# Hybrid retention and MLA block: wide modulation sets, row-tile groups of 1, 3, 5 and 7, and the norm factor applied at PSUM evacuation

## The chip, the cores and the metric

One core of one Trainium2 chip runs the whole program. The metric is device time in microseconds of one execution; a smaller number is better. Three runs of the kernel before are known, and one further execution was profiled.

## What is computed

One encoder layer for 256 tokens of width 2048, all in float32. The parts that the change touches:

```python
mod = (c_act @ ada_w[l] + ada_b[l])[:, None, :]          # c_act = silu(c), ada_w 2048 x 12288
shift_a, scale_a, gate_a, shift_f, scale_f, gate_f = jnp.split(mod, 6, axis=-1)
h = rmsnorm(x, norm1_w[l]) * (1.0 + scale_a) + shift_a
proj = h @ w_in[l]                                       # 2048 x 5184
...                                                      # retention heads and MLA heads on proj
x = x + gate_a * (jnp.concatenate([ret_out, mla_out], axis=-1) @ w_o[l])
h = rmsnorm(x, norm2_w[l]) * (1.0 + scale_f) + shift_f
x = x + gate_f * ((jax.nn.silu(h @ w_gate[l]) * (h @ w_up[l])) @ w_down[l])
return rmsnorm(x, final_norm_w)
```

The six vectors of the modulation come from one token's conditioning, so a 2048 x 12288 matrix (100.7 MB) is read for six vectors. All weights together are some 305 MB, and each is read once.

## The kernel before, in words

**Streams.** All weights lie in one HBM tensor in the order of use, and the SP queue alone issues their loads. A weight step ("w", `split_weights`, L119 to L127) loads a slab into one of six "stg" buffers (512 KB), ScalarE rounds it to a high half `whi` (L124), VectorE subtracts to get the low half `wlo` (L126), three buffers each. TensorE then makes three float32r matmuls where one would do: L132 high x high, L133 high x low, L134 low x high (`mm_tokens`).

**Modulation.** `ada_set` makes a set of up to four tiles of 128 columns for one of the six sections (SC_A is scale_a, SH_A shift_a, GT_A gate_a, and so on). Its matrix slab comes in 512 KB loads through the same six "stg" buffers ("a" steps, L185). A set goes one of two ways: on TensorE (L196: c_act, padded to 32 columns, is the stationary operand, and the 16 row tiles go to four 32-partition strips of one bank), or on VectorE (L198 and L200: one multiply-add over 128 x 512 per row tile into `ada_acc`). `finish` adds a gate's bias row (L212), `spread` sums over partitions: a gate by a matmul with ones (L218), the others by transposes (L222) and a reduction (L226), then L227 and L230 make `mod` and the gain. The string ADA_PE chooses the way set by set for SC_A and SH_A, ADA_PE2 for the sets that are needed later.

**The front.** w_in has 16 row tiles of 128. They are taken in GROUPS of 2, 4, 4 and 6, since the shift and scale of a row tile are needed before `h` of that tile can be made: while group g is projected, the modulation of group g+1 is loaded, its steps spread evenly between the weight steps (L372 to L392; LEAD says how many weight steps remain behind the last of them). `norm_x` squares x (L266), makes the factor (`rsqrt`, L114), scales x in place (L269); `turn_x` transposes it (L148) and ScalarE copies it out of PSUM (L276). `build_h1` applies gain and shift and splits (L143 to L145). Each group's `project` runs over eleven chunks of columns (CHUNKS: two PSUM banks each) and adds the chunk into SBUF accumulators (L348 copies for the first group, L350 adds for the others).

**Behind it.** The last group's chunks, MLA, retention and the output projection follow in a plan (L742 to L786) into which the loads of GT_A and of most of SC_F and SH_F are mixed, at a rate that compares an assumed DMA cost with an assumed TensorE cost (ADA_RATE, L790 to L805). Then `norm_x2` spreads the second norm factor by a small matmul (L727), the remaining SC_F and SH_F are loaded beside the first ffn chunks, and the ffn runs to the end with GT_F's modulation in between.

**Order.** `run` (L152) walks the steps and emits the loads of up to LOOK + 1 steps ahead, weights and modulation counted together. The framework then puts the instructions of each engine in an order by this priority and by its own times, with buffers from the free ones of a pool; the order is fixed before the run. The pool "big" has eight slots of 1 MB for x, its transpose, the h tiles and later tensors.

Of the kernel before, what the change touches and what calls it, by code (L numbers as in the profile page):

```python
# [85 lines left out]
def encoder_block(ctx: ExitStack, tc: tile.TileContext, x, cols, rows, pos, stream, out):  # L86
# [65 lines left out]
    def run(steps):  # L152
        ahead = [i for i, s in enumerate(steps) if s[0] != "f"]
        tiles, nxt, held = {}, 0, 0
        for i, s in enumerate(steps):
            while s[-1] not in URGENT and nxt < len(ahead) and (ahead[nxt] <= i or len(tiles) + held <= LOOK):
                j = ahead[nxt]
                kind, arg = steps[j][:2]
                tiles[j] = split_weights(arg) if kind == "w" else arg()
                nxt += 1  # L160
            if s[0] == "f":
# [12 lines left out]
    def ada_set(pool, sec, k0, nk, rowdst, on_pe):  # L174
        n = nk * P
        wide = n if not on_pe else min(n, 2 * P)
        kk = 1024 // wide
        acc = {}

        def acc_tile():  # L180
            return (pool or late["pool"]).tile([P, n], F32, name="ada_acc", tag="ada_acc", bufs=2 if pool else 1, padded_shape=[P, 512])

        def load(c, t):
            w = wp.tile([P, kk, wide], F32, name="stg", tag="stg", bufs=6)
# [3 lines left out]
        def body(c, t, w):  # L188
            if c == 0 and t == 0:
                acc["t"] = bank() if on_pe else acc_tile()  # L190
            a = acc["t"]
            for j in range(kk):
# [4 lines left out]
                elif k == 0:  # L197
                    V.tensor_scalar(out=a, in0=w[:, j], scalar1=c_act[:, 0:1], scalar2=None, op0=ALU.mult)  # L198
                else:
                    V.scalar_tensor_tensor(out=a, in0=w[:, j], scalar=c_act[:, k:k + 1], in1=a, op0=ALU.mult, op1=ALU.add)  # L200

        def finish():
# [5 lines left out]
            if rowdst is not None:  # L208
                r0 = (R_GA if sec == GT_A else R_GF) + k0 * P
                br = wp.tile([1, n], F32, name="bias_row", tag="stg", bufs=6)  # L210
                SY.dma_start(br, rows[:, r0:r0 + n])
                V.tensor_tensor(a[0:1, :], a[0:1, :], br, op=ALU.add)  # L212

        def spread():
            a = acc["a"]
            b = bank()
            if rowdst is not None:
                PE.matmul(b[:, 0:n], lhsT=ones, rhs=a, start=True, stop=True)  # L218
                S.copy(rowdst()[:, k0 * P:k0 * P + n], b[:, 0:n])
                return  # L220
# [771 lines left out]
```

## Time and profile before

| what | us |
|---|---|
| median of 3 runs | 1261.68 (1259.57 to 1261.85) |
| the profiled execution | 1259.87 |
| its span, first to last instruction | 1257.9 |
| TensorE (PE) busy | 1217.3, 97% |
| VectorE (DVE) busy | 841.1, 67% |
| ScalarE (ACT) busy | 600.9, 48% |
| DMA | 315.28 MB, mean 251 GB/s |

PE is matmuls, PEld their weight loads, SP the engine that issues the DMAs. Matmuls overlap in the pipeline, so the distance between two starts, not a matmul's duration, is its price. Times within the trace count from the first instruction.

### The profile page before, as it was taken

The numbers are of one execution on the slowest core, as the hardware profiler recorded it, in microseconds if no ns is written. First come the engines' busy times: TensorE is split into PE (matmuls) and PEld (weight loads), VectorE is DVE, ScalarE is ACT, GpSimd is POOL, SyncE is SP. The second block draws the span as 40 slices with busy tenths as digits, with TensorE's granted clock in tenths as the row PEclk, the third lists the DMA queues.
The fourth block names the chain that finished last, engine by engine and source line by source line (L and its number), as shares of the span: only waits on it lengthen the run. The fifth ranks groups of instructions, "written<-read, shape, count | busy, mean of one in ns | idle before, by whom it ended". The sixth has DMA issues, their size and how long they took to land.

```text
span 1257.9 us, 16210 instructions
## 1 busy us (share of the span) xinstructions
PE 1217.3 (97%) x6022; PEld 973.0 (77%) x6022; DVE 841.1 (67%) x1157; ACT 600.9 (48%) x812; POOL 2.2 (0%) x10
## 2 busy tenths in 40 slices
PE   5899999999999999899999999999999999999997
PEld 2676667789886787678888888888888888888885
DVE  2596988889997997885555556656655454554544
ACT  4553454545557554745444444444444443444433
POOL 0000000000000000000000000000000000000000
PEclk9999999999999999899999999999999999999999
DMA  8989898888878987897676658766775655555562
GB/s 330 324 302 310 296 326 295 291 311 298 323 243 297 319 289 268 323 356 222 218 226 225 202 170 284 235 198 212 262 224 189 218 188 197 194 191 194 191 200 85
DMA packets 88800, 315.28 MB, mean 251 GB/s; under 512 B 10249, under 2 KB 10377, under 8 KB 88209
## 3 DMA queue, kind: packets, MB, share of 16 engines
q1 hardware_dynamic: 88720, 314.24, 73.4%
q8 instruction: 47, 0.77, 0.2%
q14 instruction: 33, 0.26, 0.1%
HBM read 312.11 MB, written 2.10 MB: 250 GB/s over the span
## 4 chain that ended last, share of the span: by engine, by line
PE 85%; DVE 7%; DMA 4%; ACT 2%; issue 2%; SPq 0%; ACTq 0%; DVEq 0%
PE bank L133 25%; PE bank L134 25%; PE bank L132 25%; DMA stg<-in_stream 4%; DVE wlo L126 3%; PE bank L196 3%; PE bank L148 2%; DVE ada_acc L200 2%; ACT whi L124 1%; PE bank L625 1%; PE bank L614 1%; PE bank L513 0%; PE bank L537 0%; PE bank L512 0%; PE bank L222 0%
## 5 line engine op out<-in xcount | busy, mean ns | idle before, releaser
L126 DVE TENSOR_TENSOR wlo<-stg,whi 128x1024 fp32r<-128x1024 f32 (+2 forms) x400 | 478.8, 1199 | 331.8 <-ACT whi L124 330.3
L124 ACT CAST whi<-stg 128x1024 fp32r<-128x1024 f32 (+2 forms) x400 | 413.2, 1034 | 526.1 <-PE bank L134 411.9
L132 PE MATMUL bank<-whi,actt 128*128 128x512 f32 (+1 forms) x1184 | 457.7, 392 | 11.4 <-ACT whi L124 8.2
L133 PE MATMUL bank<-wlo,actt 128*128 128x512 f32 (+1 forms) x1184 | 460.7, 389 | 6.9 <-DVE wlo L126 6.2
L134 PE MATMUL bank<-whi,actt 128*128 128x512 f32 (+1 forms) x1184 | 458.1, 387 | 0.2 <-DVE actt L145 0.2
L132 PEld LDWEIGHTS bank<-whi,actt 128*128 128x128 f32 x1184 | 221.8, 189 | 63.6 <-ACT whi L124 12.0
L133 PEld LDWEIGHTS bank<-wlo,actt 128*128 128x128 f32 x1184 | 223.2, 189 | 61.5 <-DVE wlo L126 16.7
L134 PEld LDWEIGHTS bank<-whi,actt 128*128 128x128 f32 x1184 | 223.1, 188 | 44.8 <-DVE actt L145 0.9
L200 DVE SCALAR_TENSOR_TENSOR ada_acc<-stg,c_act,ada_acc 128x512 f32<-128x512 f32 (+1 forms) x240 | 175.3, 731 | 21.2 <-DMA stg<-in_stream 18.3
L132 PE MATMUL bank<-whi,ap 128*128 128x512 f32 x352 | 137.0, 389 | 0.0
L134 PE MATMUL bank<-whi,ap 128*128 128x512 f32 x352 | 136.9, 389 | 0.0
L133 PE MATMUL bank<-wlo,ap 128*128 128x512 f32 x352 | 136.9, 389 | 0.0
L132 PEld LDWEIGHTS bank<-whi,ap 128*128 128x128 f32 x352 | 66.1, 188 | 13.8
L133 PEld LDWEIGHTS bank<-wlo,ap 128*128 128x128 f32 x352 | 66.1, 188 | 13.7
L134 PEld LDWEIGHTS bank<-whi,ap 128*128 128x128 f32 x352 | 66.1, 188 | 13.6
L196 PE MATMUL bank<-stg,c_pad 128*32 128x256 f32 x544 | 48.6, 418 | 11.4 <-DMA stg<-in_stream 11.3
L196 PEld LDWEIGHTS bank<-stg,c_pad 128*32 128x32 f32 x544 | 13.0, 112 | 35.5 <-issue 26.7
L851 ACT ACTIVATE sgs<-bank 128x512 f32<-128x512 f32 x22 | 13.1, 597 | 10.5 <-PE bank L134 9.8
L145 DVE TENSOR_TENSOR actt<-hfull,actt 128x256 fp32r<-128x256 f32 x40 | 16.3, 419 | 2.4 <-ACT actt L144 2.3
L853 DVE TENSOR_TENSOR sgs<-bank,sgs 128x512 f32<-128x512 f32 x22 | 14.3, 683 | 0.6 <-PE bank L134 0.6
L833 DVE TENSOR_TENSOR ap<-bank,ap 128x512 fp32r<-128x512 f32 x22 | 14.1, 682 | 0.0
L226 DVE TENSOR_REDUCE mod<-bank 128x4 f32<-128x512 f32 (+3 forms) x18 | 8.0, 444 | 8.9 <-PE bank L222 8.7
(219 smaller groups left out, 708.2 us busy)
## 6 DMA issues: line engine op xcount, KB each, us to landing
stg<-in_stream SPq DMA_DIRECT2D x568, 512.0 KB, 4.4
stg<-in_stream SPq DMA_DIRECT2D x16, 288.0 KB, 3.5
stg<-in_stream SPq DMA_DIRECT2D x8, 384.0 KB
xt<-in_x SPq DMA_DIRECT2D x2, 1024.0 KB
acc_cq<-in_x SPq DMA_DIRECT2D x8, 256.0 KB, 4.7
out<-x SPq DMA_DIRECT2D x8, 256.0 KB, 2.9
acc_k<-in_rows SPq DMA_DIRECT2D x1, 1024.0 KB, 7.5
fw<-in_rows SPq DMA_DIRECT2D x1, 1024.0 KB
```

What stands on the lines that cost most here:

```text
L124: S.copy(hi, stg)
L126: V.tensor_tensor(lo, stg, hi.bitcast(F32), op=ALU.subtract)
L132: PE.matmul(o, lhsT=ah, rhs=whi, start=first, stop=False)
L133: PE.matmul(o, lhsT=ah, rhs=wlo, start=False, stop=False)
L134: PE.matmul(o, lhsT=al, rhs=whi, start=False, stop=last)
L145: V.tensor_tensor(dst[:, k, T:2 * T], tmp, dst[:, k, 0:T].bitcast(F32), op=ALU.subtract)
L148: PE.transpose(b[:, j, tb * P:(tb + 1) * P], src, ident)
L196: PE.matmul(a[q:q + 32, c:c + wide], lhsT=c_pad[:, k], rhs=w[:, j], start=c == 0 and k < 4, stop=c + wide == n and k >= KT - 4)
L200: V.scalar_tensor_tensor(out=a, in0=w[:, j], scalar=c_act[:, k:k + 1], in1=a, op0=ALU.mult, op1=ALU.add)
L833: V.tensor_tensor(ap[:, ks, T:2 * T], b, ap[:, ks, 0:T].bitcast(F32), op=ALU.subtract)
L851: S.activation(sg, o[tb], AF.Silu)
L853: V.tensor_tensor(sg, o[tb], sg, op=ALU.mult)
```

## The change

GROUPS become 1, 3, 5 and 7 row tiles. In the first three groups the chunks are WIDE: 1024 columns (four PSUM banks) and one row tile per load. The modulation of the front is given set by set: SC_A goes to TensorE, SH_A to TensorE for the first four tiles and to VectorE for the other twelve, in sets of up to seven tiles. Behind the first tile's, its loads are 640 KB to 1 MB and use free slots of the pool "big", not "stg". The look-ahead counts weights (LOOK_W = 3) and modulation (LOOK_A = 1) by themselves. Later sets have 1024 columns where they go to VectorE, and of the 40 tiles needed later all but four go there; they are placed evenly over the plan's cost. x is loaded in four pieces and transposed raw; the factor is spread over a tile `rstd_b` and multiplied in as VectorE reads PSUM. A gate's bias row is loaded into the accumulator before the first multiply-add. The sums over partitions are matmuls with one column of ones.

```diff
-GROUPS = [(0, 2), (2, 4), (6, 4), (10, 6)]
-ADA_PE = "10010100101101"
-LEAD = [1, 1, 3, 3, 3, 3, 3]
-ADA_PE2 = "010000110000"
-ADA_RATE = 0.8
-ADA_AHEAD = 0
-LOOK = 3
+GROUPS = [(0, 1), (1, 3), (4, 5), (9, 7)]
+LEAD = [1, 2, 3]
+ADA_PE2 = "000100"
+ADA_END = 0.95
+LOOK_W = 3
+LOOK_A = 1
...
-    def ada_set(pool, sec, k0, nk, rowdst, on_pe):
+    def ada_set(pool, sec, k0, nk, rowdst, on_pe, large=False):
         n = nk * P
-        wide = n if not on_pe else min(n, 2 * P)
-        kk = 1024 // wide
+        wide = n if not on_pe else P * (2 - nk % 2)
+        kk = 1 << ((2048 if large else 1024) // wide).bit_length() - 1
...
-            w = wp.tile([P, kk, wide], F32, name="stg", tag="stg", bufs=6)
+            if large:
+                w = big.tile([P, D], F32, name="astg", tag="m8")[:, 0:kk * wide].rearrange("p (k n) -> p k n", k=kk)
+            else:
+                w = wp.tile([P, kk, wide], F32, name="stg", tag="stg", bufs=6)
...
+                if not on_pe and rowdst is not None:
+                    G.memset(acc["t"], 0.0)
+                    bias_row(acc["t"])
...
             for j in range(nk):
-                PE.transpose(b[:, j * P:(j + 1) * P], a[:, j * P:(j + 1) * P], ident)
+                PE.matmul(b[:, j:j + 1], lhsT=a[:, j * P:(j + 1) * P], rhs=ones[:, 0:1], start=True, stop=True)
             ks = slice(sec * KT + k0, sec * KT + k0 + nk)
             m = mod[:, ks]
-            parts = b[:, 0:n].rearrange("p (j q) -> p j q", q=P)
-            V.tensor_reduce(out=m, in_=parts[:, :, ::32] if on_pe else parts, axis=AX.X, op=ALU.add)
-            V.tensor_tensor(m, m, col[:, C_ADAB + ks.start:C_ADAB + ks.stop], op=ALU.add)
+            V.tensor_tensor(m, b[:, 0:nk], col[:, C_ADAB + ks.start:C_ADAB + ks.stop], op=ALU.add)
...
+    S.activation(stat[:, 60:61], ones[:, 0:1], AF.Sqrt)
...
+    def spread_rstd(r):
+        b = bank()
+        for tb in range(NB):
+            dg = mid.tile([P, P], F32, name="dg", tag="hfull", bufs=2)
+            V.tensor_scalar(out=dg, in0=ident, scalar1=r[:, tb:tb + 1], scalar2=None, op0=ALU.mult)
+            PE.matmul(b[:, tb * P:(tb + 1) * P], lhsT=ones, rhs=dg, start=True, stop=True)
+        S.copy(rstd_b, b[:, 0:T])
...
-        S.copy(xnT[k // 8][:, k % 8:k % 8 + 2, :], b)
+    def scale_x(k):
+        V.tensor_tensor(xnT[k // 8][:, k % 8:k % 8 + 2, :], raw.pop(k), rstd_b.unsqueeze(1).broadcast_to([P, 2, T]), op=ALU.mult)
...
+        by = 1 if sum(widths) > CH else 2
...
+    pe_sets = [
+        [(SC_A, 1, 3), (SH_A, 1, 3)],
+        [(SC_A, 4, 4), (SC_A, 8, 1)],
+        [(SC_A, 9, 4), (SC_A, 13, 3)],
+    ]
+    dve_sets = [[], [(SH_A, 4, 5)], [(SH_A, 9, 7)]]
...
-        chunks = WIDE if nk == 1 else CHUNKS
-        ws = [w for c in chunks for w in project(gi, *c)]
+        parts = [ada_stream(mid, [(*st, None, on_pe, True) for st in sets[gi]]) for sets, on_pe in ((pe_sets, True), (dve_sets, False))]
+        order = sorted((i / len(u), n, i) for n, u in enumerate(parts) for i in range(len(u)))
+        units = [parts[n][i] for _, n, i in order]
+        ws = [w for c in WIDE for w in project(gi, *c)]
...
-    early = [(GT_A, 4 * i, 4, lambda: gate_a) for i in range(4)]
-    early += [(sec, k, min(4, K_LATE - k), None) for sec in (SC_F, SH_F) for k in range(0, K_LATE, 4)]
+    early = [(GT_A, 8 * i, 8, lambda: gate_a) for i in range(2)]
+    early += [(sec, k, min(8, K_LATE - k), None) for sec in (SC_F, SH_F) for k in range(0, K_LATE, 8)]
...
-        for _ in range(2):
-            if units and dma < pe * ADA_RATE + ADA_AHEAD:
-                steps += units.pop(0)
-                pe += 0.5
-                dma += 1.5
+        want = min(len(units), int(len(units) * done / (ADA_END * sum(cost))))
+        for u in units[used:want]:
+            steps += u
+        used = want
```

## Rows read from the trace of the kernel before

**Rows 1.** The page's chain that ended last, by engine

```profile
PE 85%; DVE 7%; DMA 4%; ACT 2%; issue 2%; SPq 0%; ACTq 0%; DVEq 0%
```

**Rows 2.** Windows by stage: us, busy us of each engine, PEclk, DMA share, GB/s

```profile
2.00:23.60 21.60, 9.91 (x72) 2.55 (x72) 5.30 (x12) 9.12 (x15) 0.74 (x2) 1.00 1.01 397
23.60:72.00 48.40, 42.47 (x233) 28.98 (x234) 27.70 (x37) 29.01 (x47) 0.00 (x0) 0.96 0.85 299
72.00:135.00 63.00, 62.66 (x334) 47.54 (x334) 50.97 (x70) 25.67 (x32) 0.00 (x0) 1.00 0.91 313
135.00:209.00 74.00, 69.76 (x376) 49.47 (x375) 64.53 (x133) 36.63 (x50) 0.00 (x0) 1.00 0.89 311
209.00:505.00 296.00, 293.66 (x1728) 236.93 (x1727) 259.72 (x455) 167.97 (x300) 0.00 (x0) 1.00 0.84 292
505.00:560.00 55.00, 50.19 (x208) 38.20 (x209) 50.93 (x74) 31.66 (x45) 0.00 (x0) 0.94 0.92 339
560.00:1258.00 698.00, 688.67 (x3078) 569.32 (x3076) 381.96 (x381) 299.62 (x328) 0.00 (x0) 1.00 0.63 207
```

**Rows 3.** Timeline of the start: start us, us, engine, line, operation, count

```profile
2.11 11.06 SPq L185 DMA_DIRECT2D stg<-in_stream  x8
...
9.12 1.91 ACT L266 ACTIVATE sq<-xt 128x2048 f32<-128x2048 f32 x1 [0.50 <-DMA xt<-in_x]
...
12.88 2.48 DVE L269 TENSOR_SCALAR xt<-xt,stat 128x2048 f32<-128x2048 f32 x2
...
14.26 1.08 PE L196 MATMUL bank<-stg,c_pad 128*32 128x256 f32 x8 [0.20 <-DMA stg<-in_stream]
...
19.38 1.08 PE L196 MATMUL bank<-stg,c_pad 128*32 128x256 f32 x8 [0.20 <-DMA stg<-in_stream]
...
23.63 0.72 PE L132 MATMUL bank<-whi,actt 128*128 128x512 f32 x1 [1.80 <-ACT actt L144]
```

**Rows 4.** Waits of the SP queue: us in total, times, longest us

```profile
SPq L122 <- DVE wlo L126: 532.6, 280, 4.2
```

**Rows 5.** Timeline of PE: starts of matmuls, 9 and 24 apart; modulation at 499.76

```profile
30.07 0.29 PE L133 MATMUL bank<-wlo,actt 128*128 128x288 f32 x1
...
31.25 0.30 PE L133 MATMUL bank<-wlo,actt 128*128 128x288 f32 x1
...
204.02 0.39 PE L134 MATMUL bank<-whi,actt 128*128 128x512 f32 x1
...
209.46 0.39 PE L134 MATMUL bank<-whi,actt 128*128 128x512 f32 x1
...
499.76 1.93 PE L196 MATMUL bank<-stg,c_pad 128*32 128x256 f32 x32
```

**Rows 6.** Groups of DVE by shape, 135 to 209: count, busy us, mean ns, idle before

```profile
L126 DVE TENSOR_TENSOR wlo<-stg,whi 128x1024 fp32r<-128x1024 f32 x19 | 23.2, 1221 | 2.4 <-ACT whi L124 2.3
L200 DVE SCALAR_TENSOR_TENSOR ada_acc<-stg,c_act,ada_acc 128x512 f32<-128x512 f32 x13 | 9.7, 747 | 0.0
L200 DVE SCALAR_TENSOR_TENSOR ada_acc<-stg,c_act,ada_acc 128x256 f32<-128x256 f32 x15 | 7.2, 482 | 0.2
...
L126 DVE TENSOR_TENSOR wlo<-stg,whi 128x576 fp32r<-128x576 f32 x4 | 2.9, 756 | 0.0
L350 DVE TENSOR_TENSOR acc_g<-acc_g,bank 128x512 f32<-128x512 f32 x4 | 2.7, 687 | 0.1
...
L350 DVE TENSOR_TENSOR acc_ck<-acc_ck,bank 128x288 f32<-128x288 f32 x4 | 1.6, 447 | 0.0
...
L226 DVE TENSOR_REDUCE mod<-bank 128x4 f32<-128x512 f32 x1 | 0.7, 692 | 0.1
```

**Rows 7.** Tile ada_acc: duration min/median/max ns of the bias add

```profile
L212 DVE TENSOR_TENSOR ada_acc<-ada_acc,bias_row x8: 659/673/674, 240.8 to 951.8; 1x512 f32<-1x512 f32 x8
```

**Rows 8.** Line L350: what its engine waited for before it, us and times

```profile
  PE bank L134: 12.2, 10
```

More of the change, by code (lines that the diff above doesn't have):

```diff
@@ L152, in run @@
     def run(steps):
-        ahead = [i for i, s in enumerate(steps) if s[0] != "f"]
+        ahead = [(i, s[0]) for i, s in enumerate(steps) if s[0] != "f"]
         tiles, nxt, held = {}, 0, 0
+        count = {"w": 0, "a": 0}
         for i, s in enumerate(steps):
[L156 to L159, printed above, removed]
+            while s[-1] not in URGENT and nxt < len(ahead):
+                j, kind = ahead[nxt]
+                if j > i and (count[kind] + (held if kind == "w" else 0) > (LOOK_W if kind == "w" else LOOK_A)):
+                    break
+                tiles[j] = split_weights(steps[j][1]) if kind == "w" else steps[j][1]()
+                count[kind] += 1
                 nxt += 1
+            if s[0] != "f":
+                count[s[0]] -= 1
             if s[0] == "f":
@@ L207, in finish @@
             acc["a"] = a
-            if rowdst is not None:
-                r0 = (R_GA if sec == GT_A else R_GF) + k0 * P
+            if on_pe and rowdst is not None:
                 br = wp.tile([1, n], F32, name="bias_row", tag="stg", bufs=6)
-                SY.dma_start(br, rows[:, r0:r0 + n])
+                bias_row(br)
                 V.tensor_tensor(a[0:1, :], a[0:1, :], br, op=ALU.add)
@@ L256, in encoder_block @@
     for tb in range(NB):
-        SY.dma_start(xt[tb], x[tb * P:(tb + 1) * P, :])
+        for u in range(2):
+            SY.dma_start(xt[tb][:, u * 1024:(u + 1) * 1024], x[tb * P:(tb + 1) * P, u * 1024:(u + 1) * 1024])
     S.activation(c_act, col[:, C_C:C_C + KT], AF.Silu)
+    S.activation(stat[:, 60:61], ones[:, 0:1], AF.Sqrt)
     G.memset(c_pad, 0.0)
@@ L293, in rotary_tables @@
         for tb in range(NB):
[L294 to L295 removed]
+            an = mid.tile([P, 2, 96], F32, name="ang", tag="dec", bufs=2)
+            a, n = an[:, 0], an[:, 1]
             V.tensor_scalar(out=a, in0=freq, scalar1=posf[:, tb:tb + 1], scalar2=None, op0=ALU.mult)
@@ L353, in project @@
         return [
-            ("w", ("w_in", k0 + kp, min(2, nk - kp), c0, sum(widths)), lambda hi, lo, kp=kp: body(kp, hi, lo))
-            for kp in range(0, nk, 2)
+            ("w", ("w_in", k0 + kp, min(by, nk - kp), c0, sum(widths)), lambda hi, lo, kp=kp: body(kp, hi, lo))
+            for kp in range(0, nk, by)
         ]
@@ L722, in norm_x2 @@
         rsqrt(stat[:, 30:32], stat[:, 28:30], 1.0 / D)
-        b = bank()
-        for tb in range(NB):
-            dg = mid.tile([P, P], F32, name="dg", tag="dg", bufs=2)
-            V.tensor_scalar(out=dg, in0=ident, scalar1=stat[:, 30 + tb:31 + tb], scalar2=None, op0=ALU.mult)
-            PE.matmul(b[:, tb * P:(tb + 1) * P], lhsT=ones, rhs=dg, start=True, stop=True)
-        S.copy(rstd_b, b[:, 0:T])
+        spread_rstd(stat[:, 30:32])
     h2 = {}
```

71 lines of the change are left out of this document (37 added, 34 removed).

## The prediction

> **What bounds the kernel now.** I read four views in this order. The chain of waits first [rows 1]: PE holds 85% of the path that sets the end, DVE 7%, DMA 4%. So the kernel is a PE kernel with holes, and the question is where the holes lie. The windows by stage say where [rows 2]: in the ffn (560 to 1258) PE is busy 688.67 of 698 us and DVE only 55%, so nothing is to be had there. The holes are in the front: 11.7 us of PE idle before 23.6, 5.9 before 72, then 0.3, 4.2, 2.3, and 4.8 between 505 and 560. There DVE is busy 57% in the first stage and 81 to 93% in the later ones, and DMA moves 292 to 339 GB/s, though the first window, with the same 512 KB loads, reaches 397 GB/s. Third, the timeline of the start [rows 3]: eight modulation loads (SC_A and SH_A of two row tiles) must land before the first projection matmul at 23.63. The last eight matmul records over them start at 19.38. Last, who holds the loads back [rows 4]: the SP queue waits for DVE's wlo subtraction 532.6 us in total, that is for a free "stg" buffer. All streamed data shares six of those. In the front neither DMA at full rate nor PE is the limit; the six buffers and DVE's pace are.
>
> **Prices.** 24 matmuls of 512 columns take 209.46 − 204.02 = 5.44 us, 0.227 each; nine of 288 columns 31.25 − 30.07 = 1.18, 0.131 each [rows 5]. One row tile of w_in is 54 of the first and 12 of the second: 13.8 us of PE. Modulation on PE: 32 records in 1.93 us are two tiles of 128 columns, 0.97 us a tile [rows 5]. On DVE: 128x256 takes 482 ns, 128x512 747, so 0.21 us plus 1.03 ns a column [rows 6]; that makes 640 columns 0.88, 896 columns 1.14 and 1024 columns 1.28 us. One row tile of w_in is 2.65 MB, one modulation tile 1.05 MB.
>
> **Part 1, the start.** Four loads instead of eight are needed, so the wait for the last falls from 19.38 to 14.26, where the fourth was being used [rows 3]: −5.1 us. The single finish, spread and scaling stay. The transposes of raw x no longer wait for the factor (one PSUM bank is held for it instead); the factor's path (squares end at 11.0 [rows 3], then some 3 us for the sum, two small DVE steps, two matmuls and two copies, about 14) lies beside the loads. It also drops the 2.48 us scaling [rows 3] and adds eight DVE evacuations of 0.69 [rows 6], all but one of them later and beside the DMA. The first tile's transposes and copy (19.38 to 23.63 holds them now) are earlier, worth about 1 us more. First projection matmul at 17.5 instead of 23.6.
>
> **Part 2, the three stages.** Before: group 0 (two tiles) 48.4 us, of which 27.6 are w_in matmuls; group 1 63 and group 2 74, each with 55.2. With the start of 23.6, 71.0 us are not w_in matmuls. PE's own need, with modulation, was 59.1 of 63 (0.94) and 61.0 of 74 (0.82): 0.88 on the mean.
>
> After, stage 0 has one tile (13.8) and needs x, 2 + 6 modulation tiles and one w_in tile: 13.1 MB. At 397 GB/s from 2.0 that is 35 us, at 313 it is 44 [rows 2]; from the last load to the first matmul of the next group another 5 (now 23.63 − 19.38 = 4.2). So 40 to 49; I take 43, nearer the fast end, since six buffers now serve the weights alone and the 1 MB loads have three or more of their own. Stage 0 lasts 25.5, 11.7 of them not w_in.
>
> Stage 1 (three tiles): PE 41.4, four tiles of modulation 3.9, and one tile in 128-column pieces. No row shows that piece: half the columns in the same count of instructions is 0.97 a tile if time goes by columns, 1.93 if by instructions; I take 1.3. Together 46.6. DVE: 16.9 + 1.9 for wlo, 16 × 0.88 = 14.1 modulation, 18 × 0.69 + 4 × 0.45 = 14.2 evacuation, 47.1 [rows 6]. DMA 18.4 MB, 46 us at 397. Stage 2 (five tiles): PE 69.0 + 3.9 + 3 × 1.3 = 76.8; DVE 31.3 + 18.2 + 14.2 + about 10 for the rotary tables, 73.7; DMA 28.0 MB, 70 us at 397. At 0.88 the stages last 53.0 and 87.3, so 11.6 and 18.3 are not w_in. Sum after: 17.5 + 11.7 + 11.6 + 18.3 = 59.1 against 71.0: **−11.9 us**. The seventh tile of the last group is w_in work that moved, not work added. Seven more weight units and the changed look-ahead I cost at nothing: DVE hides 1.1 us of fixed time, and PE has four units in hand as now; without that cover, 1.1 us.
>
> **Part 3, 209 to 505.** PE loses eight tiles of modulation, 7.7 us. DVE gains them: four wide sets and one of 512 cost 92.9 against 81.8 for seven now, less four bias adds of 0.67 [rows 7] and some 3 us of reductions (four of 0.69 [rows 6]): +5.3 us. PE is busy 293.66 of 296 there and DVE 259.72, 88% [rows 2]. If PE alone binds, −8; if DVE binds, +5. I take −4, halfway, since PE has the higher share but DVE had little left. The memset and bias load of a new accumulator stand in POOL's and SP's queues; POOL is idle, and behind SP's wait stand weight loads with four units of cover.
>
> **Part 4, 505 to 560.** DVE (50.93 of 55) loses one 0.69 reduction from the path: −1 us, between −2 and 0. The ffn stays.
>
> **Sum:** 1259.87 (span 1257.9) − 11.9 − 4 − 1 = 1243. The profiled run is 1.8 us below the median of 1261.68; I forecast on its scale. A measurement here tells about 0.2%, 2.5 us, from no change.
>
> **Rivals.** *A, PE's pace.* With separate buffers the front runs as group 1 did, 0.94 of PE's need, and stage 0 ends at 40: 49.6 + 81.7 instead of 53.0 + 87.3, and 3 less: 1231. For it: 397 GB/s was reached; against: DVE's need is within 5% of PE's. The Trainium skill's DMA: Bandwidth & Descriptors (Measured) asks for transfers of 1 MiB or more and fits 2.0 us of fixed time per DMA; by it 26 fewer loads in the front would save an estimated 52 us, which only this rival could even partly use. The trace disagrees: 512 KB loads reach 397 GB/s here [rows 2], above the 341 the page has for a lone 1 MB.
>
> *B, DMA stays at 312 GB/s.* If the single queue on SP, where a 1 MB load that waits for a slot blocks the weights behind it, keeps today's rate, 59.5 MB end at 2 + 191, plus 5: 198 instead of 183. Time 1257. For it: three stages at 299 to 313; against: they shared six buffers.
>
> *C, PSUM runs out; slower.* Each wide chunk holds four of eight banks where it held two, and modulation holds one or two more. So the next chunk must wait for the last one's first evacuation: behind a wlo (1.22) and a modulation step (0.88 to 1.14), plus 0.69 itself, 2.8 to 3.0 us, less six matmuls in the banks left, 1.4. At 15 chunk starts (five a stage) that is about 23 us: 1266. It turns the result when a start costs more than 16.9 / 15 = 1.1 us. Against it: now the evacuations wait for PE (12.2 us, ten times [rows 8]), PE never for them; and a chunk's first bank is full 2 us before its end. The Trainium skill's Perfetto Trace Analysis (Matmuls) asks that matmul groups rotate through banks so that evacuation overlaps the next group, which this change makes harder; the rows of before show no such bubble, so it stays a minor case.
>
> **Chances.** Forecast 0.52, A 0.15, B 0.21, C 0.12. The range of 1228 to 1258 takes in A with part 3 at its better end, and most of B; C and B's tail stay out. Faster: the forecast, A and about two thirds of B, 0.80; same: B's upper part, 0.08; slower: C, 0.12.
>
> **What would show it.** First projection matmul near 17.5; group 1 from about 43; the last group's first matmuls near 183; 128 fewer modulation records on PE in the stretch that is now 209 to 505. Wrong, if PE waits for acc_ evacuations (C), if DMA stays near 312 GB/s up to 183 (B), or if the first stages gain and DVE passes 90% afterwards while PE idles.

## The result and the profile after: slower, 1269.7 us

The changed kernel takes 1269.74 us (median of 6 runs, 1266.48 to 1275.37) against 1260.26 us of the kernel before on the same chip (6 runs, 1258.41 to 1261.85): a ratio of 1.008, 95% interval 1.0051 to 1.0109. The forecast of 1243 and its range of 1228 to 1258 both missed, on the side that had 12%. The profiled execution of the changed kernel took 1273.79 us with a span of 1271.7, 13.8 us more than the span before. It is one of the longer of the six: the medians differ by 9.5 us, so some 4 of the 13.8 us taken apart below belong to this execution.

The chain of waits by engine, which answers to [rows 1]:

```profile
PE 78%; DVE 10%; DMA 6%; issue 3%; ACT 3%; SPq 0%; ACTq 0%; DVEq 0%
```

TensorE holds 78% of the path instead of 85: more of the end is set by DVE and DMA. The windows by stage (us, busy us of PE, PEld, DVE, ACT and POOL, granted clock, DMA share, GB/s) answer to [rows 2]; the bounds are now the first projection matmul, the starts of groups 1, 2 and 3, and the second norm's scaling at 521.5:

```profile
2.00:20.95 18.95, 6.70 (x77) 5.18 (x77) 3.12 (x13) 10.36 (x21) 0.73 (x2) 1.00 1.01 375
20.95:52.00 31.05, 29.33 (x306) 22.56 (x306) 13.24 (x20) 19.75 (x36) 0.00 (x0) 0.95 0.76 298
52.00:110.00 58.00, 53.79 (x312) 40.22 (x311) 43.83 (x62) 19.91 (x26) 0.00 (x0) 0.94 0.84 326
110.00:198.40 88.40, 84.32 (x523) 66.86 (x522) 63.96 (x85) 36.89 (x50) 1.91 (x2) 0.98 0.81 316
198.40:521.50 323.10, 306.93 (x1695) 253.22 (x1693) 278.63 (x459) 177.48 (x317) 0.00 (x0) 0.98 0.80 277
521.50:575.00 53.50, 48.90 (x213) 39.07 (x209) 50.65 (x72) 31.56 (x45) 0.00 (x0) 0.97 0.93 349
575.00:1271.70 696.70, 687.29 (x3073) 568.88 (x3073) 379.79 (x376) 298.73 (x327) 1.58 (x3) 1.00 0.62 207
```

Nine row tiles are done at 198.4, where the kernel before had done ten at 210.5. One tile is 13.8 us of PE, so on the scale of before the front ends at 212.2: 1.7 us later, where 11.9 earlier was forecast. From there to the second norm ("the middle") it takes 323.1 us, or 309.3 without the seventh tile, against 295.5 before (210.5 to 506.0): 13.8 us longer, where 4 shorter was forecast. The rest, from 521.5 on, is 1.7 us shorter (750.2 against 751.9), as forecast. 1.7 + 13.8 − 1.7 is the whole difference.

In the middle PE idles 323.1 − 306.9 = 16.2 us; before it idled 2.3 (busy 293.2 of 295.5):

```profile
210.50:506.00 295.50, 293.16 (x1733) 236.22 (x1731) 258.24 (x452) 167.28 (x300) 0.00 (x0) 1.00 0.84 293
```

PE's busy time without the extra tile, 306.9 − 13.8 = 293.1, did not fall, though modulation on PE fell from 20.4 to 9.6 us. The next view shows part of the reason: the first 67 us of the middle in PE's waits (us, times, longest), and the windows where the clock fell.

```profile
PE bank L131 <- ACT whi L123: 4.3, 2, 3.4
PE bank L132 <- DVE wlo L125: 3.1, 4, 1.4
```
```profile
222.00:226.00 4.00, 1.73 (x14) 1.50 (x12) 4.00 (x8) 0.88 (x3) 0.00 (x0) 1.00 0.90 281
226.00:230.00 4.00, 2.79 (x6) 1.80 (x7) 2.90 (x10) 3.90 (x6) 0.00 (x0) 0.51 1.01 407
230.00:234.00 4.00, 4.00 (x13) 3.17 (x12) 4.00 (x11) 1.35 (x3) 0.00 (x0) 0.64 1.01 376
```

PE waits for weight halves, and after it has worked 1.73 of 4 us the granted clock goes to 0.51 (1.2 GHz): the same matmuls then count as more busy time. Over the whole middle the clock is at this lower level for 13.7 us, which is 6.8 us of full speed lost; in the middle of the kernel before it never is (1.00 in the row above).

### The profile page after: what moved, and what is told of

It reads as the page before. It is cut to its first block, busy times and chain, and to the rows that moved or that the text cites. A ratio compares the mean times of both kernels' runs of the same rounds, so it can differ in the third digit from the quotient of the medians.

```text
span 1271.7 us, 16448 instructions
## 1 busy us (share of the span) xinstructions
PE 1217.3 (96%) x6186; PEld 996.0 (78%) x6186; DVE 833.2 (66%) x1082; ACT 596.0 (47%) x817; POOL 5.7 (0%) x15
## 4 chain that ended last, share of the span: by engine, by line
PE 78%; DVE 10%; DMA 6%; issue 3%; ACT 3%; SPq 0%; ACTq 0%; DVEq 0%
PE bank L132 24%; PE bank L133 23%; PE bank L131 23%; DMA stg<-in_stream 5%; DVE wlo L125 4%; DVE ada_acc L211 2%; PE bank L207 2%; PE bank L147 2%; ACT whi L123 1%; PE bank L238 1%; DMA xt<-in_x 1%; PE bank L233 0%; PE bank L665 0%; PE bank L654 0%; DVE acc_q L386 0%
## 5 line engine op out<-in xcount | busy, mean ns | idle before, releaser
L125 DVE TENSOR_TENSOR wlo<-stg,whi 128x1024 fp32r<-128x1024 f32 (+3 forms) x407 | 478.4, 1180 | 328.4 <-ACT whi L123 321.5
L123 ACT CAST whi<-stg 128x1024 fp32r<-128x1024 f32 (+3 forms) x407 | 413.6, 1019 | 545.8 <-PE bank L133 436.1
L132 PE MATMUL bank<-wlo,actt 128*128 128x512 f32 (+1 forms) x1184 | 463.6, 392 | 14.0 <-DVE wlo L125 13.8
L211 DVE SCALAR_TENSOR_TENSOR ada_acc<-stg,c_act,ada_acc 128x512 f32<-128x512 f32 (+1 forms) x155 | 148.9, 961 | 30.3 <-DMA stg<-in_stream 27.9
L133 PEld LDWEIGHTS bank<-whi,ap 128*128 128x128 f32 x352 | 66.1, 188 | 13.8
L131 PEld LDWEIGHTS bank<-whi,ap 128*128 128x128 f32 x352 | 66.1, 188 | 13.6
L132 PEld LDWEIGHTS bank<-wlo,ap 128*128 128x128 f32 x352 | 66.1, 188 | 13.6
L211 DVE SCALAR_TENSOR_TENSOR ada_acc<-astg,c_act,ada_acc 128x640 f32<-128x640 f32 (+1 forms) x30 | 30.4, 1014 | 0.3
L207 PE MATMUL bank<-astg,c_pad 128*32 128x128 f32 (+1 forms) x448 | 21.2, 322 | 0.0
L238 PEld LDWEIGHTS bank<-ones,ada_acc 128*128 128x128 f32 x128 | 16.3, 191 | 4.8 <-issue 2.4
L207 PEld LDWEIGHTS bank<-astg,c_pad 128*32 128x32 f32 x448 | 12.3, 114 | 8.3 <-issue 6.3
L238 PE MATMUL bank<-ones,ada_acc 128*128 128x1 f32 x128 | 15.8, 244 | 2.3 <-DVE ada_acc L211 1.1
```

What stands on the lines that cost most here:

```text
L123: S.copy(hi, stg)
L125: V.tensor_tensor(lo, stg, hi.bitcast(F32), op=ALU.subtract)
L131: PE.matmul(o, lhsT=ah, rhs=whi, start=first, stop=False)
L132: PE.matmul(o, lhsT=ah, rhs=wlo, start=False, stop=False)
L133: PE.matmul(o, lhsT=al, rhs=whi, start=False, stop=last)
L207: PE.matmul(a[q:q + 32, c:c + wide], lhsT=c_pad[:, k], rhs=w[:, j], start=c == 0 and k < 4, stop=c + wide == n and k >= KT - 4)
```

## The experiments

All ratios come from runs beside the kernel before. "Front" is where the last addition before the last group ends; "middle" is from there to the second norm's scaling, both from the profile. Runs with groups 1, 3, 5, 7 are put on the scale of before (front + 13.8, middle − 13.8). Front and middle are those of one execution each. Profiles of near-equal kernels differ by some 2 us in the front, and executions of one kernel differ in all: the six of the changed kernel by 8.9 us, and e15's profiled one is 5.1 us above its median. A middle that differs by a few us settles nothing unless the ratio says the same.

| run | what it is | front | middle | ratio to before, interval |
|---|---|---|---|---|
| before | | 210.5 | 295.5 | 1 |
| after | the change | 212.2 | 309.3 | 1.0080 (1.0051 to 1.0109) |
| e1 | after, small modulation loads in the front | 222.9 | 304.4 | 1.0169 (1.0142 to 1.0196) |
| e2 | after, old sets and pacing | 210.8 | 321.4 | 1.0220 (1.0196 to 1.0243) |
| e3 | after, old sets | 210.4 | 310.0 | 1.0125 (1.0103 to 1.0147) |
| e5 | after, joint look-ahead | 213.9 | 308.7 | 1.0123 (1.0101 to 1.0144) |
| e6 | after, rotary tables early | 208.7 | 304.9 | 1.0065 (1.0048 to 1.0083) |
| e7 | after, transposes instead of the column of ones | 209.0 | 309.3 | 1.0063 (1.0045 to 1.0082) |
| e8 | after, start reordered | 210.6 | 306.7 | 1.0086 (1.0068 to 1.0104) |
| e9 | after, old groups | 207.2 | 306.0 | 1.0047 (1.0033 to 1.0061) |
| e10 | after, old sets, pacing, look-ahead; rotary early | 212.0 | 321.2 | 1.0227 (1.0203 to 1.0250) |
| e11 | as e10 with old groups | 205.9 | 305.1 | 1.0057 (1.0038 to 1.0076) |
| e12 | after, chunks of 512 in stages 1 and 2 | 215.0 | 304.9 | 1.0096 (1.0076 to 1.0115) |
| e13 | before, chunks of 1024 | 219.1 | 295.4 | 1.0075 (1.0053 to 1.0097) |
| e14 | after, stage 2's sets in turn | 216.9 | 307.8 | 1.0105 (1.0088 to 1.0122) |
| e15 | as e14, rotary early | 214.4 | 305.7 | 1.0063 (1.0040 to 1.0085) |
| e16 | before, with the start and large loads of the change | 210.4 | 296.6 | 0.9998 (0.9986 to 1.0010) |
| e17 | as e11, stage 2's sets in turn | 209.5 | 307.8 | 1.0052 (1.0036 to 1.0067) |
| e18 | before, with the column of ones alone | 219.4 | 310.5 | 1.0187 (1.0168 to 1.0205) |
| e19 | as e17, with transposes | 209.3 | 294.2 | 0.9975 (0.9962 to 0.9988) |

### Undoing one part: e1, e2, e3, e5

```diff
# e1
-(*st, None, on_pe, True) for st in sets[gi]
+(*st, None, on_pe, False) for st in sets[gi]
# e3 (e2 has the old pacing too)
-ADA_PE2 = "000100"
+ADA_PE2 = "010000110000"
-    early = [(GT_A, 8 * i, 8, lambda: gate_a) for i in range(2)]
+    early = [(GT_A, 4 * i, 4, lambda: gate_a) for i in range(4)]
...
# e5
-                if j > i and (count[kind] + (held if kind == "w" else 0) > (LOOK_W if kind == "w" else LOOK_A)):
+                if j > i and len(tiles) + held > LOOK_W:
```

> The changed kernel with one thing undone: the front's modulation loads are at most 512 KB again and go through the six shared stg buffers, not through free slots of the pool big. Theory F (in the front the SP queue waits for a free 1 MB slot, with weight loads stuck behind it, and then the 1 MB loads issued in a burst crowd the weights out): the DMA hole of about 8 us before 50 us and PE's wait near 54 to 66 us go, the last group starts near 185 to 190 us instead of 198, and the whole is 8 to 13 us faster, about 1258 to 1262. Rival F2 (the front is bound by PE's and DVE's work, and the holes only move): within 3 us of the changed kernel, about 1267 to 1272. Second rival (sharing six buffers is what held the front back before): slower than the changed kernel by 5 us or more.

Theory F, that the kernel would gain, fell; the second rival held. The front is 10.7 us longer without the large loads and their own slots: with these groups that part of the change works. The middle is shorter by 5.0, less than the front lost.

> The changed kernel with the later modulation sets as they were before: 512 columns, three of ten sets on TensorE, and the old pacing by assumed DMA and TensorE cost. Front, start and look-ahead stay as changed. Theory M (the 12 us lost between the start of the last group and norm_x2 come from what was done to these sets): the stretch from 198 to 520 us shrinks by 9 to 13 us, total 1257 to 1262. Rival L (they come from the separate look-ahead of weights and modulation, whose six outstanding loads fill all six stg buffers): within 3 us of the changed kernel, 1267 to 1272.

> As the run before it in this batch, but the new even pacing is kept: only the sets are 512 columns wide again, with three of ten on TensorE. If the width and the move from TensorE to VectorE are the cause: like that run, 9 to 13 us faster than the changed kernel. If the pacing is: within 3 us of the changed kernel. If the look-ahead is: both runs within 3 us of the changed kernel.

> The changed kernel with the old rule of the look-ahead: weights and modulation counted together, at most four loads ahead. Rival L (six loads outstanding fill the six buffers): 5 to 12 us faster than the changed kernel, most of it between 198 and 520 us. Theory M (the sets): within 3 us. In the front theory F expects little: the astg loads still wait for their slots, perhaps 0 to 4 us faster, since fewer of them stand ahead of the weights.

None of the three brings the middle back, and their ratios are 0.4 to 1.4% above that of the changed kernel (those of e3 and e5 with intervals that just overlap it). The old pacing makes the middle 11 us longer than the old sets alone do (321.4 against 310.0). None of these parts is the cause alone, as long as the rest stays.

### The hand-over, the spread, the start and the groups: e6 to e9

In the changed kernel, SyncE's issues at the end of stage 2 (start us, us, line, operation) have two gaps:

```profile
194.13 0.35 SPq L193 DMA_DIRECT2D stg<-in_stream  x1
194.57 0.24 SPq L215 DMA_DIRECT2D ada_acc<-in_rows  x1
200.01 0.33 SPq L121 DMA_DIRECT2D stg<-in_stream  x1
...
201.75 0.33 SPq L193 DMA_DIRECT2D stg<-in_stream  x1
207.62 0.33 SPq L121 DMA_DIRECT2D stg<-in_stream  x1
```

Behind the second stands VectorE with the rotary tables, two of whose 13 lines are:

```profile
202.49 1.10 DVE L336 SCALAR_TENSOR_TENSOR ang<-ang 128x96 f32<-128x96 f32 x6
...
206.07 0.33 DVE L341 TENSOR_SCALAR sc_t<-ang 128x96 f32<-128x96 f32 x2
```

```diff
# e6
-        if gi == 2:
+        if gi == 0:
             steps.append(f(rotary_tables))
# e8
-    S.activation(stat[:, 60:61], ones[:, 0:1], AF.Sqrt)
+    S.activation(stat[:, 60:61], c_act[:, 0:1], AF.Sqrt, scale=0.0)
...
-    steps += [f(scale_x, 0), f(build_h1, 0)]
+    steps += [f(spread_x), f(scale_x, 0), f(build_h1, 0)]
# e9
-GROUPS = [(0, 1), (1, 3), (4, 5), (9, 7)]
+GROUPS = [(0, 2), (2, 4), (6, 4), (10, 6)]
```

> The rotary tables are listed after stage 0 instead of after stage 2, nothing else changes. In the changed kernel their 30-odd small VectorE operations and two table loads run at 201 to 206 us, at the head of the last group, where VectorE is busy 62.98 of 67 us and TensorE waits 8.4 us; in the kernel before they ran at 143 to 165 among other work. Theory R (the tables' place costs the middle): they move to a stretch before 198, TensorE's waits between 198 and 265 fall from 8.4 to about 3, the stretch from the last group's start to the second norm falls from 323 to 317, and the time is 1265. Rival G (the seven-tile last group with VectorE sets of 1024 columns makes VectorE late, tables or not): the waits move to another place of the same stretch, that stretch stays at 321 to 324, and the time is 1270 to 1274.

The middle is 4.4 us shorter, though PE still waits 6.8 us in its first 67, where theory R had about 3. The ratio falls only from 1.0080 to 1.0065, and the two intervals overlap, so this run alone shows no gain; e15 below repeats it.

> A modulation set becomes columns as before the change: one TensorE transpose a tile and a VectorE sum over it, instead of one matmul with a column of ones. Theory S (the column of ones costs more than a transpose, 16 records 1.88 us against 4 records 0.59 us, and TensorE is on the path): TensorE loses about 6 us of work over the whole run, 2.5 of it after 198, and the time falls by 3 to 6 us, to 1266 to 1269. Rival V (TensorE waits for VectorE there, and the sums come back onto VectorE at 0.6 us for four tiles): no change within 2 us, or up to 3 us slower, 1270 to 1275.

The spread's own PE time falls from 15.8 to 10.8 us over the run, but the middle does not move. The median, 1268.5, lies in the range of theory S, and the gain of 1 to 2 us is what rival V allows, so this run does not decide between them. Its profiled execution is the longest of its six (1262.77 to 1269.68). This run matters again below: it is the change without the column of ones, its middle is still 309.3, and it is still 0.6% slower than the kernel before.

> At the start the square-root table is loaded after Silu's (its input is now Silu's output, times 0), and the two matmuls that spread the norm factor are listed after the modulation's 64 records, not before. Theory O (the start lost 3.5 us to this order): no table load stands in front of the norm's square root at 11.4 us, the modulation's records run before 14.6 us, and the first projection matmul starts at 17.5 to 18.5 us instead of 20.95. What the rest makes of it: if the weights' transfers set the end of stage 0, the gain is lost there (that stage ends at 52 as before) and the time stays at 1270 to 1273; if TensorE sets it, the time is 1267 to 1269.

Theory O fell. Its rows on PE, first the modulation, then the spread and the norm factor, then the first projection matmul:

```profile
15.68 1.08 PE L207 MATMUL bank<-stg,c_pad 128*32 128x128 f32 x16
17.15 0.59 PE L238 MATMUL bank<-ones,ada_acc 128*128 128x1 f32 x2 [0.39 <-ACT ada_acc L221]
17.59 1.20 PE L285 MATMUL bank<-dg,ones 128*128 128x128 f32 x4
21.11 0.79 PE L131 MATMUL bank<-whi,actt 128*128 128x512 f32 x1 [2.31 <-ACT actt L143]
```

The modulation now ends at 16.8 instead of 18.1, but the factor comes behind it, and its copy, the scaling and the split of the first tile take the 3.5 us from 17.59 to 21.11 one after another.

> Groups of 2, 4, 4, 6 row tiles as before the change, with everything else of the changed kernel (large modulation loads, raw x transposed, column of ones, sets of 1024, separate look-ahead, new pacing). Ten tiles are then done before the last group as in the kernel before, so the marks compare directly: last group's start 210.5 before, its start to the second norm 295.5. Theory G (the middle lost its 13 us to the seven-tile group: more split steps, and the single odd tile at each chunk's end): the middle takes 296 to 300, the front ends at 206 to 212, and the time is 1256 to 1262. Rival M (the middle lost it to the new sets, pacing and spread, whatever the group's size): the middle takes 305 to 310 and the time is 1267 to 1273.

The front is 5 us shorter than with the new groups (207.2 against 212.2) and the middle 3.3: by the middle that is rival M, most of the loss is not the seven-tile group. The time, 1266.0, lies between the two forecasts.

### The middle as a whole, the chunks, and the hand-over: e10 to e15

e10 joins e2, e5 and e6, e11 adds e9; e12 and e13 change the width of the front's chunks, e14 and e15 let stage 2's modulation run as four tiles and then three.

```diff
# e12
-        ws = [w for c in WIDE for w in project(gi, *c)]
+        ws = [w for c in (WIDE if nk == 1 else CHUNKS) for w in project(gi, *c)]
# e13, in the kernel before
-        chunks = WIDE if nk == 1 else CHUNKS
+        chunks = WIDE
# e14
+        if gi == 2:
+            parts = [ada_stream(mid, [(sec, k, n, None, sec == SC_A, True) for k, n in ((9, 4), (13, 3)) for sec in (SH_A, SC_A)])]
```

> The changed kernel with all of the middle's schedule put back at once (sets of 512 columns with the old choice of engine, the old pacing, one look-ahead of four for weights and modulation together) and the rotary tables listed after stage 0; the front (groups 1, 3, 5, 7, chunks of 1024 columns, large loads) and the column of ones stay. Theory M (the schedule of the middle as a whole loses the time, its parts only together): the stretch from the last group's start to the second norm falls from 323 to about 309, which is the 295.5 of the kernel before and one row tile more, and the time is 1255 to 1259. Theory W (the loss begins at the hand-over to the last group: the front's chunks of 1024 columns put four additions behind one another at their end, the weight splits of the last group wait behind them on VectorE, the slots of the weight ring with them, and SyncE issues nothing for 5 us): the stretch stays at 317 or more, and the time is 1265 to 1275.

> As the run with the middle's schedule of before, and with the groups of before (2, 4, 4, 6) as well; what is left of the change is raw x transposed, large modulation loads, chunks of 1024 columns in the front, and the column of ones. Theory M: front 207 as with the old groups alone, middle 296 to 298, time 1252 to 1256, faster than the kernel before. Theory W: middle 303 or more, time 1260 to 1267.

> One edit in the changed kernel: stages 1 and 2 take their weights as chunks of 512 columns by two tiles, as before the change, instead of 1024 by one tile. Theory W: two additions instead of four end a chunk, the weight splits of the last group run before the stage's last additions as they did before the change, SyncE has no gap of 5 us between 190 and 200, TensorE's waits in the first 67 us of the last group fall from 8.4 to 2 or 3, the middle falls from 323 to 312 to 316, and the time is 1260 to 1265. Theory M: the middle stays at 320 to 324 and the time at 1268 to 1274.

> One edit in the kernel before: the three stages take w_in as chunks of 1024 columns by one tile. Theory W: the gap in SyncE's issues comes with the wide chunks, the middle rises from 295.5 to 302 to 306, and the time is 1264 to 1270. Theory M: the middle stays within 2 us of 295.5 and the time is 1256 to 1262.

Theory M fell with e10 and e11: with the whole schedule of the middle put back, its length is 321.2 and 305.1. Theory W fits e11 but fell with e13: in the kernel before, wide chunks cost the front 8.6 us and the middle nothing; its time, 1267.2, is in W's range only through the front. In e12 the middle is 4.4 us shorter and the front 2.8 longer, and the ratio does not fall.

> One edit in the changed kernel: in stage 2 the modulation sets run one after another, four tiles and then three, shift and scale in turn, as in the kernel before, instead of one seven-tile set of the shift on VectorE beside the scale on TensorE. Theory H (the hand-over: because the seven-tile set ends with the stage, all 14 ScalarE operations that build the last group stand in one block at 189 to 198 us, the last group's weight splits behind them, and SyncE issues nothing from 194.6 to 200.0): the first four tiles are built 15 us or more before the stage's end, that gap goes, TensorE's waits in the next 67 us fall from 8.4 to 5, and the middle falls from 323 to 317 to 319; the time is 1263 to 1267. Rival D (VectorE's load in the middle makes the waits, whatever stands at the hand-over): the middle stays at 321 to 324 and the time at 1268 to 1273. By theory H the second gap, 201.75 to 207.62 behind the rotary tables, stays.

> As the run with the sets in turn, and the rotary tables listed after stage 0. Theory H: both gaps of SyncE at the hand-over go, TensorE's waits in the first 67 us of the last group are 2 to 3 us, as in the kernel before, the middle takes 311 to 314 (295.5 and one tile of 13.8 make 309, and the waits late in the middle stay) and the time is 1257 to 1261. Rival D: no more than the 4 us that the tables' move gave alone, middle 318 to 320, time 1266.

In e14 SyncE's longest gap between 190 and 200 us is 2.9 us (197.14 to 200.01) instead of 5.4, as theory H has it, but the middle is only 1.5 us shorter and the front 4.7 longer. Around its own hand-over, at 203.1, there is one of 4.6 (205.05 to 209.62). The first gap goes and most of the loss stays, so that gap is not the cause of the whole. In e15 the tables' early place again brings a few us (2.1 in the middle, 2.5 in the front), and here the ratio says so too: 1.0105 in e14, 1.0063 in e15.

### What all of these kept: e16 to e19

Every run so far that was slow in the middle, bar e7, had the column of ones.

```diff
# e18, in the kernel before
-                PE.transpose(b[:, j * P:(j + 1) * P], a[:, j * P:(j + 1) * P], ident)
+                PE.matmul(b[:, j:j + 1], lhsT=a[:, j * P:(j + 1) * P], rhs=ones[:, 0:1], start=True, stop=True)
...
-            V.tensor_reduce(out=m, in_=parts[:, :, ::32] if on_pe else parts, axis=AX.X, op=ALU.add)
-            V.tensor_tensor(m, m, col[:, C_ADAB + ks.start:C_ADAB + ks.stop], op=ALU.add)
+            V.tensor_tensor(m, b[:, 0:nk], col[:, C_ADAB + ks.start:C_ADAB + ks.stop], op=ALU.add)
# e19, from e17: the same lines back
```

> The kernel before with what seems worth keeping: large modulation loads in the front, raw x transposed with the norm factor applied behind it, x loaded in halves, the square-root table asked for early, rotary tables after stage 0. Groups of 2, 4, 4, 6, chunks of 512 columns, sets of 512, old pacing and look-ahead and the spread by transposes are as before. Theory H: the front ends at 200 to 206 instead of 210.5, the middle takes 296 to 299, and the time is 1248 to 1256. Rival: the large loads, issued earlier, leave the last group's first weights late again, the middle takes 303 or more, and the time is 1258 to 1264.

The middle is back at 296.6, and so is the front at 210.4: the time is that of before within 0.2%. Theory H had the front at 200 to 206. Beside the old groups and chunks of 512, the large loads and the new start gain nothing.

> The run with the groups and the middle's schedule of before (front 206, middle 305.1), and stage 2's sets in turn, four tiles and then two, instead of one six-tile set of the shift on VectorE. Theory H: no stretch of 6 us without an issue on SyncE at the hand-over, the middle falls from 305.1 to 297 to 300, and the time is 1257 to 1260. Rival D: the middle stays within 2 us of 305 and the time at 1264 to 1267.

Rival D: 307.8. Between e17 and e16 lie the column of ones, the wide chunks and the lead.

> One edit in the kernel before: a modulation set becomes columns through a matmul with a column of ones instead of a transpose and a VectorE sum. Theory C (the column of ones is what costs the middle 10 us, through the order of the work around it, beyond the 2 us of TensorE that its records take there): the stretch from the last group's start to the second norm rises from 295.5 to 303 to 308, the front stays at 210, and the time is 1264 to 1270. Theory W (the wide chunks of the front cost it): the middle is 295 to 298, and the time is 1257 to 1262.

> The run e17 (groups of 2, 4, 4, 6, the middle's schedule of before, stage 2's sets in turn, chunks of 1024 columns in the front) with the spread by transposes and sums as before. Theory C: the middle falls from 308.4 to 296 to 299, the front stays at 209, and the time is 1255 to 1259. Theory W: the middle stays at 304 to 309 and the time at 1263 to 1268.

Theory C holds in both directions for the middle. The column of ones alone makes the kernel before 1.9% slower, the middle by 15.0 and the front by 8.9 us; taken out of e17 it gives back 13.6 us of the middle. Its size was off in e18: the front was to stay and the time to be 1264 to 1270, and 1282.4 was measured. The 8.9 us of front do not come back in e19 (209.5 and 209.3), so what they need besides the column of ones is open. **e19 beats both kernels**: 1255.84 us, 0.25% under the kernel before.

The whole middle of e18, to be held against that of the kernel before (293.16 busy of 295.50):

```profile
219.40:529.90 310.50, 301.52 (x1755) 240.87 (x1753) 261.67 (x485) 171.44 (x306) 0.00 (x0) 0.99 0.79 280
```

Why so much? First its own price on PE, from e18 (line, operation, count, busy us, mean ns, idle before it):

```profile
L222 PE MATMUL bank<-ones,ada_acc 128*128 128x1 f32 x128 | 17.0, 252 | 2.8 <-DVE ada_acc L200 2.3 <-ACT ada_acc L206 0.5
```

and from e19:

```profile
L242 PE MATMUL bank<-ident,ada_acc 128*128 128x128 f32 x64 | 10.6, 278 | 0.6 <-ACT ada_acc L221 0.5
```

One column of output takes two matmul records a tile, 128 against 64, and 15.8 (after) to 17.0 us of PE against 10.6: 5 to 6 us over the run, some 2 in the middle. That is not 15. The rest seems to lie in the order of the work. Here is what VectorE does with the set that is spread behind 400 us, and when it begins the next one, in the kernel before:

```profile
400.67 0.15 DVE L227 TENSOR_TENSOR mod<-mod,col 128x4 f32<-128x4 f32 x1
...
415.35 0.46 DVE L198 TENSOR_SCALAR ada_acc<-stg,c_act 128x512 f32<-128x512 f32 x1
```

and in e18:

```profile
415.68 0.16 DVE L225 TENSOR_TENSOR mod<-bank,col 128x4 f32<-128x4 f32 x1 [2.47 <-PE bank L222]
...
439.17 0.48 DVE L198 TENSOR_SCALAR ada_acc<-stg,c_act 128x512 f32<-128x512 f32 x1
```

From the set's columns to the next set's first step it is 14.7 us before and 23.5 in e18; e19 and e17 repeat the pair to the digit (398.26 to 412.94, 401.11 to 424.60). With the column of ones the instructions of each engine come out in another order: VectorE stands 2.47 us before PE's result, and other work goes ahead of the next modulation set. SyncE has issued 98 modulation loads by 400 us in e19 and 97 in e17, by 420 us 107 and 103: four are put off. Not all of the 13.6 us arise at this set. The `wlo` subtraction of the same number starts 0.2 us later in e17 than in e19 at 217 us, 2.7 at 237, 2.1 at 365, 10.5 at 446 and 13.8 at 513, so some 8 us come around the set shown and 5 or 6 in two other places. The windows of the whole middle, e17 and then e19:

```profile
209.50:517.30 307.80, 300.73 (x1755) 242.14 (x1754) 254.96 (x447) 167.16 (x300) 0.53 (x1) 0.98 0.80 281
```
```profile
209.30:503.50 294.20, 290.88 (x1723) 235.78 (x1722) 257.64 (x453) 166.59 (x300) 0.52 (x1) 1.00 0.83 294
```

PE waits 7.1 us in e17 and 3.3 in e19, and its busy time is 9.9 us longer at a mean clock of 0.98 instead of 1.00. Of the 9.9, 2.2 are the spread's records (6.1 against 3.9), 1.2 are modulation records that lie ahead of the window in e19 (248 against 256), and 5.1 are what the clock takes: it is at its lower level for 10.2 us of e17's middle and for none of e19's. Some 1.4 stay without a name. The same matmuls count as longer, one line of them in e17 and in e19:

```profile
L133 PE MATMUL bank<-whi,actt 128*128 128x512 f32 (+1 forms) x258 | 100.9, 391 | 0.0
```
```profile
L133 PE MATMUL bank<-whi,actt 128*128 128x512 f32 (+1 forms) x258 | 98.8, 383 | 0.0
```

That the order is what costs, and not something else in those records, is argued from these rows; no run kept the old order with the column of ones. Nor did a run change the order with an edit that has no work of its own, so how far any new order moves the time is not known; e13, an edit of the chunk width alone, moved the front by 8.6 us.

**What stays open.** e18 shows that the column of ones is enough by itself to lengthen the middle by 15 us. e7 shows that the rest of the change is enough without it: 309.3 again. The two do not add, and with old groups, old middle and transposes (e16, e19) nothing is left. How the second part divides between the sets of 1024 columns, the pacing, the look-ahead and the groups wasn't measured, since the runs that undid those (e2, e3, e5, e9, e10, e11) kept the column of ones, which may have hidden it. The tables' place is some 2 to 4 us of it (e6, e15). So what made the changed kernel's own middle longer is shown only in part.

## Why the prediction was wrong

**Part 1, the start** (17.5 forecast, 20.95 measured). The loads did land early, as the step said. What failed is "its path lies beside the loads": on PE's queue the norm factor's matmuls stand ahead of the modulation and wait for VectorE, so the 64 modulation records start at 14.62 and run 3.5 us, that is 1.75 for 32 where the later pieces of the same shape take 1.08. In the chain before them ScalarE loads the square-root table again at 11.40, for 1.28 us: the early request had run before that of Silu.

```profile
13.47 1.22 PE L285 MATMUL bank<-dg,ones 128*128 128x128 f32 x4 [3.66 <-DVE dg L284]
14.62 3.50 PE L207 MATMUL bank<-stg,c_pad 128*32 128x128 f32 x64
18.06 0.85 PE L238 MATMUL bank<-ones,ada_acc 128*128 128x1 f32 x4
20.95 0.54 PE L131 MATMUL bank<-whi,actt 128*128 128x512 f32 x1 [2.04 <-ACT actt L143]
```

e8 shows that neither order gives 17.5: the small steps from the last spread to the first matmul are a chain of 2.9 to 3.5 us.

**Part 2, the stages** (−11.9 forecast with the start, +1.7 measured). What is not w_in matmul was 17.2, 16.6 and 19.4 us in the three stages instead of 11.7, 11.6 and 18.3. In stage 0 the step that failed is "the 1 MB loads have three or more of their own". This is rival B, which said that the front would end at 198 instead of 183: it ended at 198.4, with 298, 326 and 316 GB/s in the three stages. That is one fact and not two, since the bytes are nearly the same and a stage that is long for any reason has a low rate; in stages 1 and 2 PE was busy 93 and 95% of the time. B's mechanism is seen in stage 0: SyncE waits 9.3 us at once (us, times, longest) for a slot that the projection still reads, and the weights stand behind it:

```profile
SPq L193 <- PE bank L133: 9.3, 1, 9.3
```
```profile
39.77 0.42 SPq L121 DMA_DIRECT2D stg<-in_stream  x1
49.59 0.33 SPq L193 DMA_DIRECT2D astg<-in_stream  x1
```
```profile
44.00:48.00 4.00, 2.91 (x32) 2.40 (x21) 2.56 (x4) 3.21 (x6) 0.00 (x0) 1.00 0.02 4
```

Between 44 and 48 us the DMA moves 4 GB/s. In stage 1 PE then waits 4.2 us for low halves. There the step that failed is PE's need of 46.6: PE was busy 53.8 us, with 2.4 for the column of ones (20 records), which the need left out, and a clock of 0.94, which is 3.5 of 58 us. The large loads themselves are worth 10.7 us of front with these groups (e1); the groups took part of it back, since with the old ones the front is 5 us shorter (e9). The wide chunks, taken as free but for rival C, cost the front 8.6 us alone (e13); in the changed kernel, undoing them in stages 1 and 2 made it 2.8 longer (e12). The piece of 128 columns on PE, taken at 1.3 us a tile, measured 1.08 for its 32 records at a granted clock of 1.00, near the bound by columns. The prediction quoted the Trainium skill's DMA: Bandwidth & Descriptors for a fixed 2.0 us a load; that fit stands in its section Anatomy of one DMA — SWDGE (gpsimd) path, for DMAs that GpSimd issues, and here SyncE issues them. e1 has 34 more loads than the changed kernel and a front 10.7 us longer, 0.3 us a load, and part of that may come from the six buffers that its loads share again: the direction agrees, the size does not.

**Part 3, the middle** (−4 forecast, +13.8 measured). Three steps failed. The column of ones was never priced on PE: the prediction only credited VectorE with 3 us of reductions, and took the order of each engine's work as given. Put into the kernel before, it costs 15.0 us of middle (e18); taken out of the changed kernel it gives back nothing of the middle (e7), so it is enough for such a loss but is not the only cause here. The rotary tables were counted in stage 2 with about 10 us; they took 4.8 us of VectorE and ran behind the stage, at 201.6 to 206.4. And "between −8 and +5 by PE's or VectorE's share" assumed an even load: VectorE's sum grew to 278.63, 86% of the stretch, but it was 62.98 of the first 67 us, where PE waits 8.4 (first row); before, it was 54.48 and PE waited 1.7 (second row):

```profile
198.40:265.40 67.00, 58.59 (x333) 49.83 (x332) 62.98 (x121) 37.39 (x67) 0.00 (x0) 0.95 0.83 280
```
```profile
210.50:277.50 67.00, 65.28 (x412) 52.07 (x411) 54.48 (x97) 36.38 (x66) 0.00 (x0) 1.00 0.86 302
```

The prediction's last sentence on what would prove it wrong names half of this, VectorE past 90% while PE idles; its other half, a gain in the first stages, did not come. Its term for PE, −7.7, was right as work (modulation 20.4 to 9.6) and was given back as idle time (13.9 us more than before), as matmuls at the lower clock and as the spreads' own 1.9 us. How much of the idle time belongs to which part of the change stays open.

**Part 4** (−1 forecast, −1.7 measured) was right as a number. The reason, one reduction less on VectorE, is not shown: e7 has the reduction back, and its stretch from the second norm's scaling on is as short (749.6).

**The rivals.** A fell: PE was busy 0.93 to 0.95 of each stage, as A had it, but at the lower clock and with spreads that A's need lacked, and stage 0 ended at 52, not 40. B was right for the front and silent on the middle. C gave the right side and nearly the time, 1266, by luck, for the wrong reason: PE's waits between 21 and 198 us are 8.3 us for low halves, 2.0 for the first tile's split, 1.1 for a spread and 0.4 for a high half, and none for an evacuation of an accumulator, so the rotation of banks that the Trainium skill's Perfetto Trace Analysis (Matmuls) asks for was not what this change lacked.

## What to carry to other kernels

Price an operation that replaces another at its place in each engine's queue, not only by its duration: a spread that saves VectorE at most 0.69 us a set [rows 6] came with a next set 9 us later and 23 us in all (e18). When several parts of a change each cost time by lateness, undoing one at a time may show nothing, as here; put one part alone into the kernel before, and take it out of the best version, as e18 and e19 do. Judge an engine's load by the worst stretch, not by the stage's mean.

## What the runs showed of the hardware that was not expected

A float32 matmul with a single column of output is two records of some 250 ns with a weight load each, 0.24 to 0.26 us of PE a tile in a row (four tiles in 0.95 to 1.05), where a transpose of the same 128x128 tile takes 0.15 to 0.17 (four in 0.60 to 0.66). A short wait on PE can be paid twice: in e17's middle 3.8 us more of idle time than in e19 came with 10.2 us at the lower clock, 5.1 us more for the same matmuls. And the large loads land 8.5 to 9.8 us after their issue (medians), those of 640 KB no sooner than those of 1 MB (9.8 and 9.6), the 512 KB loads of the whole run after 4.4, on the one queue that all use.
